# Two transformer blocks on one core: weight items split in halves, the joined product form kept for the FFN ups alone, the recurrence in bursts of four, and two block boundaries with reordered TensorE work

## The chip, the core and the metric

One Trainium2 chip, one core. The metric is device time in microseconds (us) of one execution; the time before is the median of three runs. TensorE runs the matrix products, VectorE (DVE) and ScalarE (ACT) the elementwise work, and the queues of SyncE (SP), ACT and GpSimd (POOL) start DMA transfers.

## The reference, cut to what matters

Two blocks run one behind the other on 256 tokens of width 2048. Block 2 puts 16 meta tokens ahead, so that it has 272 until its attention. Left out here are the normalisations' details, the spatial gating, the pooling and the softmax.

```python
def first_block(x, c, ...):
    mod = silu(c) @ w_ada + b_ada                      # six vectors of 2048
    h = rms_norm(x, g_pre_mix) * (1 + sc1) + sh1
    y = token_mixing(h, w_in, ..., w_out)              # gMLP, attention, pooling
    x = x + gt1 * rms_norm(y, g_post_mix)              # boundary 1
    h = rms_norm(x, g_pre_ffn) * (1 + sc2) + sh2
    y = conv_ffn(h, w_up, w_conv, b_conv, w_down)      # w_up: 2048 x 11264
    return x + gt2 * rms_norm(y, g_post_ffn)           # boundary 2

def second_block(x, meta_tokens, ...):
    h = concatenate([meta, x])
    z = rms_norm_2(h, norm_mix) @ w_in
    q_lat, kv_lat, k_r, u, gates = split(z)
    attn = mla_attention(...)                          # 16 heads, causal
    attn_out = attn @ w_attn_proj                      # w_ap in the kernel
    y = gelu(s5_scan(u, ...))                          # linear recurrence over tokens
    ssm_out = (y @ w_glu_val) * sigmoid(y @ w_glu_gate)
    h = h + (sigmoid(g0) * attn_out + sigmoid(g1) * ssm_out) @ w_out   # boundary 3
    m = rms_norm_2(h, norm_ffn)
    h = h + (silu(m @ w_ffn_gate) * (m @ w_ffn_up)) @ w_ffn_down
    return rms_norm_2(h, norm_final)[:, N_META:]
```

## The kernel before

**Products.** Every fp32 operand is held as a pair, a rounded high part and the rest: a weight is `wh`, `wl`, an activation `act[:, 0]`, `act[:, 1]`. A product is then three: high by high, high by low, low by high. `mm3` (L354) issues three products of 256 columns (L362 to L364; 272 where the meta tokens are in). `mm2` (L366) takes the two with `wh` as one product of 512 columns (L376) and the third as 256 (L378); its two halves of the result have to be added afterwards, by `join` (L380: an ACT copy L382, a DVE add L383). `mmtok` (L386, L394 to L396) has the tokens as rows of the result and 512 columns. `group_unit` and `single_unit` use `mm2`, for the FFN ups of both blocks and for `w_ap`.

**Weights.** A weight item is 1 MB (128 x 2048; some are smaller). SP loads it into one of nine `raw` buffers (L222). `split_piece` (L226) makes the pair: ACT writes `wh` (L249), of which there are four buffers, and DVE `wl` (L250). It does so in two halves of 128 x 1024, or, where the flag `whole` is set, in one piece of 128 x 2048. The flag is set in `block1_in` (L855) and stays set, so nearly all items after the first part of block 1 are split whole.

**Order.** Nothing chooses an order at run time: the program is emitted unit by unit in `run_units` (L322), and every engine does its instructions in that order. A unit (16 values of k by one item, mostly) emits its products, then four stages. Each stage moves the evacuations of the units before by one step (`advance`) and may emit one `split_piece`, in the first two stages only if `whole` is set. Items are split three ahead (`ahead_to`). After the stages two lists of generators are moved on, `side` and `bg`; they carry the attention, the recurrence of s5 and other small work beside the products.

**Boundaries.** At the end of a residual block `tok_block` with `half` (L1080 to L1093) forms the product for the first 128 tokens (a = 0), then for the second (a = 1). Ahead of the evacuation of one of them it splits items of the next stage, `1 + a` of them (L1086). `residual` (L1156) normalises, adds, and for a = 1 returns `dg` (L483), a diagonal of the inverse norms. The next stage's input is made by `lazy_t` (L491), k by k as the first products ask for it: a transpose of the first half (L504), a product of the second with `dg` (L506), at boundary 2 a product of 16 columns for the meta tokens (L508), and then ACT (L512, or L745, L746, L748) and DVE (L513, or L749, L750) write the pair. Boundary 1 is the passage into the first FFN, boundary 2 that into block 2, boundary 3 that into the second FFN.

**The recurrence and its outputs.** 66 steps of eight small DVE operations (L1810 to L1817) run as a `bg` generator that yields after every second step (L1818). Its outputs are PE products of 64 columns (L1846 to L1848), a gelu on ACT (L1852), stores to and loads from DRAM on ACT's queue (L1856, L1863) and a split (L1872, L1873). Attention is emitted by `side` generators in between; its exponentials are L1548, its products L1533, L1534, L1563, L1565 and L1576 to L1578.

```python
                for s in range(stages):
                    self.advance()
                    if self.split < goal and (s < 2 or not self.whole):
                        self.split_piece(self.whole)
```

## Time and profile before

| | |
|---|---|
| median of three runs | 3018.43 us (3017.03 to 3022.11) |
| profiled execution: time, span | 3019.66 us, 3017.9 us |
| PE busy, mean granted clock | 2929.5 us (97% of the span), 0.98 |
| DVE, ACT busy | 2005.8 us (66%), 1391.6 us (46%) |
| matmuls | 17836 |
| HBM read | 632.42 MB, 218 GB/s over the span |
| chain that ended last | PE 92%, DVE 3%, DMA 2%, ACT 2%, issue 1% |

PE is busy nearly throughout and is most of the chain that ended last. The time that could go lies in three places: what the products themselves take, the stretches in which PE stands idle, and those in which the granted clock of TensorE is lower. The granted clock is printed as a share of the full speed: 1.00 is 2.4 GHz, 0.50 is 1.2 GHz.

### The profile page before, as it was taken

How to read it: one execution, taken by the hardware profiler on the slowest of the kernel's cores; microseconds unless marked ns; L12 is line 12 of the kernel's file. 1: busy time of each engine (PE TensorE's matmuls, PEld its weight loads, DVE VectorE, ACT ScalarE, POOL GpSimd, SP SyncE). 2: the span in 40 equal slices, each digit the busy share in tenths (PEclk: the TensorE clock that was granted, in tenths of full speed). 3: DMA queues.
4: the chain of work that ended last, by engine and by line, in shares of the span. 5: the costliest groups of instructions: out<-in, count | busy, mean ns of one | idle time of the engine just before them, and what ended most of it. 6: DMA issues, size and time to landing. Idle time of an engine off the chain costs nothing.

```text
span 3017.9 us, 43503 instructions
## 1 busy us (share of the span) xinstructions
PE 2929.5 (97%) x17836; PEld 2593.5 (86%) x17836; DVE 2005.8 (66%) x2959; ACT 1391.6 (46%) x1878; POOL 56.9 (2%) x109
## 2 busy tenths in 40 slices
PE   6999999989999999999899998999999999999998
PEld 4999989878888888888899996789888888888887
DVE  6889888868779788676436773545645555555454
ACT  4545434456545555455444334434445434444343
POOL 0000000000000100000000000000000000000000
PEclk9999999999999999999899999899999999999999
DMA  9987778775567677556465664246644555555553
GB/s 355 348 302 277 276 269 335 296 257 182 193 241 271 230 268 255 203 180 214 143 220 191 212 209 138 84 162 217 228 179 173 182 198 186 197 183 186 193 190 129
DMA packets 127224, 660.48 MB, mean 219 GB/s; under 512 B 23009, under 2 KB 36065, under 8 KB 57393
## 3 DMA queue, kind: packets, MB, share of 16 engines
q1 hardware_dynamic: 86258, 603.30, 56.0%
q10 hardware_dynamic: 34464, 35.47, 3.7%
q0 software_dynamic: 6304, 18.95, 1.7%
q8 instruction: 140, 2.29, 0.3%
q14 instruction: 58, 0.48, 0.1%
HBM read 632.42 MB, written 25.23 MB: 218 GB/s over the span
## 4 chain that ended last, share of the span: by engine, by line
PE 92%; DVE 3%; DMA 2%; ACT 2%; issue 1%; ACTq 0%; SPq 0%; DVEq 0%
PE pm L376 23%; PE pm L378 12%; PE pm L362 9%; PE pm L363 9%; PE pm L364 9%; PE pm L394 8%; PE pm L396 8%; PE pm L395 8%; DVE wl L250 1%; ACT wh L249 1%; PE pd L506 1%; PE pd L1796 0%; PE pd L1534 0%; PE pd L1732 0%; DMA raw<-w_ada 0%
## 5 line engine op out<-in xcount | busy, mean ns | idle before, releaser
L250 DVE TENSOR_TENSOR wl<-raw,wh 128x2048 fp32r<-128x2048 f32 (+3 forms) x548 | 1092.9, 2006 | 554.1 <-ACT wh L249 553.7
L376 PE MATMUL pm<-act,wh 128*128 128x512 f32 x3072 | 1082.0, 395 | 3.6 <-DVE act L411 2.9
L249 ACT ACTIVATE wh<-raw 128x2048 fp32r<-128x2048 f32 (+3 forms) x548 | 913.2, 1680 | 276.1 <-PE pm L395 148.6
L378 PE MATMUL pm<-act,wl 128*128 128x256 f32 x3072 | 864.4, 281 | 0.0
L362 PE MATMUL pm<-act,wh 128*128 128x256 f32 (+1 forms) x2400 | 690.5, 288 | 8.7 <-DVE hp L842 6.3
L376 PEld LDWEIGHTS pm<-act,wh 128*128 128x128 f32 x3072 | 577.3, 188 | 136.0 <-DVE act L411 3.5
L363 PE MATMUL pm<-act,wh 128*128 128x256 f32 (+1 forms) x2400 | 685.9, 286 | 0.4 <-DVE act L750 0.3
L364 PE MATMUL pm<-act,wl 128*128 128x256 f32 (+1 forms) x2400 | 683.8, 285 | 1.4 <-DVE wl L250 1.4
L378 PEld LDWEIGHTS pm<-act,wl 128*128 128x128 f32 x3072 | 580.2, 189 | 1.2 <-issue 0.7
L362 PEld LDWEIGHTS pm<-act,wh 128*128 128x128 f32 x2400 | 461.0, 192 | 17.8 <-DVE hp L842 6.7
L363 PEld LDWEIGHTS pm<-act,wh 128*128 128x128 f32 x2400 | 460.6, 192 | 1.5 <-DVE act L750 0.7
L364 PEld LDWEIGHTS pm<-act,wl 128*128 128x128 f32 x2400 | 458.8, 191 | 1.8 <-DVE wl L250 1.8
L394 PE MATMUL pm<-wh,act 128*128 128x512 f32 (+1 forms) x1072 | 428.3, 400 | 11.3 <-ACT act L748 5.0
L396 PE MATMUL pm<-wl,act 128*128 128x512 f32 (+1 forms) x1072 | 423.8, 395 | 0.0
L395 PE MATMUL pm<-wh,act 128*128 128x512 f32 (+1 forms) x1072 | 422.8, 394 | 0.8 <-DVE act L750 0.8
L394 PEld LDWEIGHTS pm<-wh,act 128*128 128x128 f32 (+1 forms) x1072 | 201.4, 188 | 62.4 <-ACT act L748 5.6
L395 PEld LDWEIGHTS pm<-wh,act 128*128 128x128 f32 (+1 forms) x1072 | 201.9, 188 | 49.6 <-DVE act L750 1.8
L396 PEld LDWEIGHTS pm<-wl,act 128*128 128x128 f32 (+1 forms) x1072 | 201.3, 188 | 48.6 <-DVE wl L250 0.4
L557 DVE SCALAR_TENSOR_TENSOR raw<-raw,cond 128x2048 f32<-128x2048 f32 x96 | 219.2, 2287 | 5.0 <-DMA raw<-w_ada 4.9
L382 ACT ACTIVATE hp<-pm 128x256 f32<-128x256 f32 x192 | 73.4, 383 | 321.5 <-PE pm L378 320.7
L383 DVE TENSOR_TENSOR hp<-hp,pm 128x256 f32<-128x256 f32 x192 | 80.4, 420 | 115.4 <-ACT hp L382 115.3
L400 ACT ACTIVATE act<-hp 128x256 fp32r<-128x256 f32 x88 | 36.4, 413 | 132.0 <-DVE hp L2025 112.9
(328 smaller groups left out, 1736.9 us busy)
## 6 DMA issues: line engine op xcount, KB each, us to landing
raw<-w_ada SPq DMA_DIRECT2D x96, 1024.0 KB, 5.9
raw<-w_up SPq DMA_DIRECT2D x88, 1024.0 KB, 4.9
raw<-w_ff SPq DMA_DIRECT2D x88, 1024.0 KB, 4.8
raw<-w_in SPq DMA_DIRECT2D x81, 1024.0 KB, 5.2
raw<-w_st SPq DMA_DIRECT2D x37, 1024.0 KB, 6.0
raw<-w_out SPq DMA_DIRECT2D x32, 1024.0 KB, 5.1
raw<-w_down SPq DMA_DIRECT2D x32, 1024.0 KB, 5.0
raw<-w_fd SPq DMA_DIRECT2D x32, 1024.0 KB, 4.9
```

Of the source, the lines that this page charges most:

```text
L249: nc.scalar.activation(vh[:, ks], r[:, ks], AF.Copy)
L250: nc.vector.tensor_tensor(vl[:, ks], r[:, ks], vh[:, ks], op=OP.subtract)
L362: nc.tensor.matmul(o, wh[:, kw, c], x[:, 0, sl], start=start, stop=False, skip_group_check=True)
L363: nc.tensor.matmul(o, wh[:, kw, c], x[:, 1, sl], start=False, stop=False, skip_group_check=True)
L364: nc.tensor.matmul(o, wl[:, kw, c], x[:, 0, sl], start=False, stop=stop, skip_group_check=True)
L376: nc.tensor.matmul(p.rearrange("p (a t) -> p a t", a=2), wh[:, kw, c], x, start=start, stop=False, skip_group_check=True)
L378: nc.tensor.matmul(p[:, T:], wl[:, kw, c], x[:, 0], start=False, stop=stop, skip_group_check=True)
L383: self.nc.vector.tensor_tensor(o, o, p[:, :T], op=OP.add)
L394: nc.tensor.matmul(o, x[:, 0, tok], wh[:, kw], start=start, stop=False, skip_group_check=True)
L395: nc.tensor.matmul(o, x[:, 1, tok], wh[:, kw], start=False, stop=False, skip_group_check=True)
L396: nc.tensor.matmul(o, x[:, 0, tok], wl[:, kw], start=False, stop=stop, skip_group_check=True)
L557: self.nc.vector.scalar_tensor_tensor(o, o, 0.5, self.cond, op0=OP.mult, op1=OP.mult, accum_out=self.m(seg, n))
```

## The change

- `whole` is never set, so every item is split in two halves, and in all four stages of a unit. In the program DVE and ACT have 928 halves of 128 x 1024 each in place of 112, and none of the 392 pieces of 128 x 2048; with the 1536-wide items 408 more instructions on each.
- `mm2` with `join` stays for the FFN ups (`joint=True`). The 16 items of `w_ap` go to `mm3`: 256 pairs of products become 256 triples, 16 joins (ACT and DVE) go, and the gate takes the product from PSUM.
- At the boundaries `tok_block` splits one item ahead of the evacuation, not `1 + a`. Where there are four weight items (boundaries 1 and 3) this is one item in place of two ahead of the second half's evacuation; `group_unit` then splits the next item after its first product.
- `lazy_t` first issues (in `begin`) the transposes of the first half for k = 0 to 2, the sixteen meta products into one tile (with one DVE multiply, and later per k a copy and a subtraction of 16 columns), and `fill` products whose result nothing reads: 20 at boundary 1, none elsewhere. Only then come the products that need `dg`.
- The recurrence yields after every fourth step: 17 bursts of 32 DVE operations in place of 33 of 16. With that its output products are emitted beside units 786 to 799 of the program, which are gate units with 16 values of k, and not beside 803 to 816; attention starts at unit 810 in both.

```diff
--- before.py
+++ after.py
@@ -488,32 +488,61 @@
         q = self.pg(n="jk")[:m, :src.shape[-1]]
         self.nc.scalar.activation(q, src, AF.Square, accum_out=s[:m, col:col + 1])
 
-    def lazy_t(self, src, dg, scale, bias, meta=None):
+    def lazy_t(self, src, dg, scale, bias, meta=None, fill=0):
 
         nc = self.nc
         off = 0 if meta is None else NM
         t = T + off
-        pend, made = {}, {}
+        ps, made, mt = {}, {}, {}
+        def half(k, a):
+            if k not in ps:
+                ps[k] = self.pss()
+            o = ps[k][:, a * 128:a * 128 + 128]
+            i = src[a][k // 4][:, (k % 4) * 128:(k % 4) * 128 + 128]
+            if dg[a] is None:
+                nc.tensor.transpose(o, i, self.ident)
+            else:
+                nc.tensor.matmul(o, i, dg[a], start=True, stop=True, skip_group_check=True)
+        def begin():
+            for k in range(3):
+                half(k, 0)
+            p = self.pss()
+            if meta is not None:
+                for k in range(16):
+                    nc.tensor.matmul(p[:, k * NM:k * NM + NM],
+                                     meta[0][k // 4][:NM, (k % 4) * 128:(k % 4) * 128 + 128], meta[1],
+                                     start=True, stop=True, skip_group_check=True)
+                mt[0] = self.hp(n="mt")[:, :16 * NM].rearrange("p (k t) -> p k t", k=16)
+                nc.vector.tensor_tensor(mt[0], p[:, :16 * NM].rearrange("p (k t) -> p k t", k=16),
+                                        self.vs("norm_mix", 0, 16)[:, :, None].to_broadcast([128, 16, NM]),
+                                        op=OP.mult)
+            w = self.fill_w
+            for _ in range(fill):
+                nc.tensor.matmul(p, w[:, 0, :128], w[:, 0], start=True, stop=True, skip_group_check=True)
 
         def tr(k):
-            p = self.pss()
+            if k == 0:
+                begin()
             for a in range(2):
-                o = p[:, off + a * 128:off + a * 128 + 128]
-                i = src[a][k // 4][:, (k % 4) * 128:(k % 4) * 128 + 128]
-                if dg[a] is None:
-                    nc.tensor.transpose(o, i, self.ident)
-                else:
-                    nc.tensor.matmul(o, i, dg[a], start=True, stop=True, skip_group_check=True)
+                if a or k > 2:
+                    half(k, a)
+            p = ps.pop(k)[:, :T]
+            xt = self.act_tile(t)
             if meta is not None:
-                nc.tensor.matmul(p[:, :NM], meta[0][k // 4][:NM, (k % 4) * 128:(k % 4) * 128 + 128], meta[1],
-                                 start=True, stop=True, skip_group_check=True)
-            xt = self.act_tile(t)
+                nc.vector.tensor_copy(xt[:, 0, :NM], mt[0][:, k])
+                nc.vector.tensor_tensor(xt[:, 1, :NM], mt[0][:, k], xt[:, 0, :NM], op=OP.subtract)
             if bias is None:
-                nc.scalar.activation(xt[:, 0], p[:, :t], AF.Copy, scale=scale(k))
-                nc.vector.scalar_tensor_tensor(xt[:, 1], p[:, :t], scale(k), xt[:, 0].bitcast(FT),
+                nc.scalar.activation(xt[:, 0, off:], p, AF.Copy, scale=scale(k))
+                nc.vector.scalar_tensor_tensor(xt[:, 1, off:], p, scale(k), xt[:, 0, off:].bitcast(FT),
                                                op0=OP.mult, op1=OP.subtract)
             else:
-                self.affine_split(xt, p[:, :t], scale(k), bias(k), k)
+                self.affine_split(xt, p, scale(k), bias(k), k)
+            if k == 15:
+                mt.clear()
             made[k] = xt
 
         def X(k):
@@ -852,7 +881,6 @@
             sprinkle((0.2, 0.6, 0.4)[place])
 
         tm, tp = [None] * 16, [None] * 16
-        self.call(lambda: setattr(self, "whole", True))
 
         def gates(store, base, n4, pump=1):
             for n in range(n4 * 4, n4 * 4 + 4):
@@ -1030,7 +1058,7 @@
                              lambda h: self.q[h // 2] is not None and self.k[h // 2] is not None
                              and None not in self.vatt)
 
-    def group_unit(self, items, X, K, fns, t=T, more=(11, 13)):
+    def group_unit(self, items, X, K, fns, t=T, more=(11, 13), joint=False):
 
 
         lag = 3
@@ -1039,7 +1067,7 @@
             ps = [self.psm() for _ in items]
 
             def mm(i, j):
-                if t == T:
+                if joint:
                     self.mm2(ps[i], self.wt[items[i]], X, j, j == 0, j == K - 1)
                 else:
                     self.mm3(ps[i][:, :t], self.wt[items[i]], X, j, j == 0, j == K - 1)
@@ -1059,11 +1087,14 @@
             return [fn(p) for p, fn in zip(ps, fns)]
         self.unit(items[:1], f, ahead=4)
 
-    def single_unit(self, item, X, K, fn):
+    def single_unit(self, item, X, K, fn, joint=False):
         def f(w):
             p = self.psm()
             for k in range(K):
-                self.mm2(p, w, X, k, k == 0, k == K - 1)
+                if joint:
+                    self.mm2(p, w, X, k, k == 0, k == K - 1)
+                else:
+                    self.mm3(p[:, :T], w, X, k, k == 0, k == K - 1)
             return fn(p)
         self.unit([item], f)
 
@@ -1083,13 +1114,15 @@
                     p = self.psm()
                     tok(ws, ks, a, p)
                     if (a == 1) == (len(ws) == 4):
-                        self.split_to(self.ahead_to(self.split, 1 + a))
+                        self.split_to(self.ahead_to(self.split, 1))
                     self.flush()
                     for _ in fn(a, p):
                         pass
                     half(a)
                 if self.X is not None:
+                    self.fill_w = ws[-1][0]
                     self.X(0)
+                    self.fill_w = None
             self.unit([self.add_item(ap) for ap in items], g, flush=True)
             return
         for i, (ap, kr) in enumerate(zip(items, ks)):
@@ -1184,7 +1217,8 @@
             nc.vector.scalar_tensor_tensor(self.A2, self.mod[:, 64:80], 1.0, self.vs("g_pre_ffn", 0, 16),
                                            op0=OP.add, op1=OP.mult)
         else:
-            self.X, self.made = self.lazy_t(self.x, [None, dg], lambda k: self.A2[:, k:k + 1], lambda k: self.m(3, k))
+            self.X, self.made = self.lazy_t(self.x, [None, dg], lambda k: self.A2[:, k:k + 1], lambda k: self.m(3, k),
+                                            fill=20)
             self.x = self.y = None
 
     def ffn(self, w_up, w_down, upfn, acts, start, evac, tail, late, half):
@@ -1200,9 +1234,9 @@
             if c == 0:
                 n0 = 3
                 self.call(start)
-                self.group_unit(its[:3], X, 16, [upfn(i) for i in range(3)])
+                self.group_unit(its[:3], X, 16, [upfn(i) for i in range(3)], joint=True)
             for i in range(n0, 22):
-                self.single_unit(its[i], X, 16, upfn(c * 22 + i))
+                self.single_unit(its[i], X, 16, upfn(c * 22 + i), joint=True)
                 if c == 3 and i % 5 == 4:
                     self.call(lambda b=i // 5: late(b))
             if c == 3:
@@ -1815,7 +1849,7 @@
             tt(ci, ci, tm[2], op=OP.add)
             tt(cr, cr, tm[1], op=OP.subtract)
             tt(ci, ci, tm[3], op=OP.add)
-            if c % 2:
+            if c % 4 == 3:
                 yield
         self.yS = self.dp.tile([1024, 4, 64], FT, name="yS")
         mts = {}
@@ -1947,11 +1981,8 @@
                         gload(i)
                 if n + 3 < 16:
                     gload(n + 3)
-                v = self.join(p)
-                yield
                 s = gt.pop(n)
-                nc.vector.scalar_tensor_tensor(s, s, 1.0, v, op0=OP.add, op1=OP.mult)
-                v = None
+                nc.vector.scalar_tensor_tensor(s, s, 1.0, p[:, :T], op0=OP.add, op1=OP.mult)
                 yield
                 nc.vector.scalar_tensor_tensor(self.m2[n], self.m2[n], 0.5, s, op0=OP.mult, op1=OP.add)
                 done.add(n)
```

How the instructions stand, at three places. On PE at boundary 1, before (L394 to L396 end block 1; `pd` is the PSUM tile of a transposed k, `x` and `y` the two halves of the tokens; L376 is the FFN's first product):

```order
L395 MATMUL pm_6414<-wh_6312,act_5839 128x512
L396 MATMUL pm_6414<-wl_6313,act_5839 128x512
L504 MATMUL pd_6510<-ident,x_5993 128x128
L506 MATMUL pd_6510<-dg_6508,y_5991 128x128
L504 MATMUL pd_6518<-ident,x_5993 128x128
L506 MATMUL pd_6518<-dg_6508,y_5991 128x128
L504 MATMUL pd_6526<-ident,x_5993 128x128
L506 MATMUL pd_6526<-dg_6508,y_5991 128x128
L376 MATMUL pm_6534<-act_6513,wh_6465 128x512
L378 MATMUL pm_6534<-act_6513,wl_6466 128x256
```

and now (L506 is the transpose, L508 the product with `dg`, L525 the unread product):

```order
L395 MATMUL pm_6526<-wh_6424,act_5927 128x512
L396 MATMUL pm_6526<-wl_6425,act_5927 128x512
L506 MATMUL pd_6614<-ident,x_6089 128x128
L506 MATMUL pd_6616<-ident,x_6089 128x128
L506 MATMUL pd_6618<-ident,x_6089 128x128
L525 MATMUL pd_6620<-wh_6424 128x512 x20
L508 MATMUL pd_6614<-dg_6612,y_6085 128x128
L508 MATMUL pd_6616<-dg_6612,y_6085 128x128
L508 MATMUL pd_6618<-dg_6612,y_6085 128x128
L376 MATMUL pm_6659<-act_6642,wh_6577 128x512
L378 MATMUL pm_6659<-act_6642,wl_6578 128x256
```

The three transposes and 20 products of 512 columns stand ahead of the first instruction that needs `dg`; before, one transpose did.

On PE at boundary 2, before (`me` holds the meta tokens, L362 to L364 are the first item's products):

```order
L504 MATMUL pd_13227<-ident,x_12744 128x128
L506 MATMUL pd_13227<-dg_13225,y_12856 128x128
L508 MATMUL pd_13227<-dg_13128,me_12760 128x16
L504 MATMUL pd_13234<-ident,x_12744 128x128
L506 MATMUL pd_13234<-dg_13225,y_12856 128x128
L508 MATMUL pd_13234<-dg_13128,me_12760 128x16
L504 MATMUL pd_13241<-ident,x_12744 128x128
L506 MATMUL pd_13241<-dg_13225,y_12856 128x128
L508 MATMUL pd_13241<-dg_13128,me_12760 128x16
L362 MATMUL pm_13248<-act_13231,wh_13112 128x272
L363 MATMUL pm_13248<-act_13231,wh_13112 128x272
L364 MATMUL pm_13248<-act_13231,wl_13113 128x272
```

and now (L516 is the meta product):

```order
L506 MATMUL pd_13624<-ident,x_13123 128x128
L506 MATMUL pd_13626<-ident,x_13123 128x128
L506 MATMUL pd_13628<-ident,x_13123 128x128
L516 MATMUL pd_13630<-dg_13525,me_13139 128x16 x4
L516 MATMUL pd_13630<-dg_13525,me_13140 128x16 x4
L516 MATMUL pd_13630<-dg_13525,me_13141 128x16 x4
L516 MATMUL pd_13630<-dg_13525,me_13142 128x16 x4
L508 MATMUL pd_13624<-dg_13622,y_13239 128x128
L508 MATMUL pd_13626<-dg_13622,y_13239 128x128
L508 MATMUL pd_13628<-dg_13622,y_13239 128x128
L362 MATMUL pm_13667<-act_13650,wh_13509 128x272
L363 MATMUL pm_13667<-act_13650,wh_13509 128x272
L364 MATMUL pm_13667<-act_13650,wl_13510 128x272
L506 MATMUL pd_13681<-ident,x_13123 128x128
```

The meta products left the three per-k groups ahead of the first product and, with thirteen more, the groups between the products; all sixteen stand ahead of `dg`.

On ACT beside attention, before (`yt` is an output of the recurrence, `sm` the scores, `qk` an evacuation of queries or keys, `hp` and `pt` other evacuations):

```order
L1852 ACT_TABLE_LOAD
L1852 ACTIVATE yt_17383<-yt_17383 128x512
L1485 ACTIVATE qk_17501<-pm_17488 128x256
L1580 ACTIVATE hp_17507<-pd_17503 128x256
L1567 ACTIVATE pt_17517<-pd_17510 128x384
L1548 ACT_TABLE_LOAD
L1548 ACTIVATE sm_17529,sm_17531<-sm_17529,sm_17531 128x144
L1548 ACTIVATE sm_17529,sm_17531<-sm_17529,sm_17531 128x272
L1856 DMA yS<-yt_17383 32x8x64 x4
```

and now, where attention's exponentials begin (L1906 is the former L1872, L1519 the former L1485, L1582 the former L1548):

```order
L1906 ACTIVATE act_17894<-yD_17862 128x256
L1906 ACTIVATE act_17897<-yD_17864 128x256
L1906 ACTIVATE act_17900<-yD_17866 128x256
L1519 ACTIVATE qk_17916<-pm_17903 128x272
L249 ACTIVATE wh_17920<-raw_17677 128x1024 x2
L1519 ACTIVATE qk_17939<-pm_17926 128x272
L1519 ACTIVATE qk_17954<-pm_17941 128x272
L1519 ACTIVATE qk_17969<-pm_17956 128x272
L1547 ACTIVATE vv_17984<-pm_17971 16x512
L249 ACTIVATE wh_17988<-raw_17778 128x1024 x2
L1582 ACT_TABLE_LOAD
L1582 ACTIVATE sm_17999,sm_18001<-sm_17999,sm_18001 128x144
```

The gelu and its two table loads no longer lie between exponentials; the last s5 work (`act<-yD`) is issued before the first exponential.

## Rows read from the trace of the kernel before

**Rows 1.** The page's first part: busy time, share of the span, instructions per engine.

```profile
PE 2929.5 (97%) x17836; PEld 2593.5 (86%) x17836; DVE 2005.8 (66%) x2959; ACT 1391.6 (46%) x1878; POOL 56.9 (2%) x109
```

**Rows 2.** The waits of PE: who waited for whom, us in total, times, longest.

```profile
PE pd L506 <- DVE dg L483: 18.1, 3, 8.3
PE pm L362 <- DVE hp L842: 6.3, 2, 3.3
PE pm L362 <- DVE pt L842: 1.5, 2, 0.8
```

**Rows 3.** Busy time by stretch: start:end, length, PE, PEld, DVE, ACT, POOL busy, PEclk, DMA share, GB/s.

```profile
668.50:673.10 4.60, 4.05 (x15) 3.60 (x16) 2.37 (x5) 2.32 (x5) 1.74 (x4) 0.50 0.44 131
1448.70:1471.90 23.20, 23.19 (x88) 20.57 (x89) 8.51 (x13) 7.60 (x13) 0.00 (x0) 0.50 0.16 57
1782.50:1792.70 10.20, 7.59 (x36) 7.59 (x36) 9.93 (x37) 0.00 (x0) 0.00 (x0) 0.50 0.78 284
1837.10:1850.70 13.60, 12.11 (x39) 8.46 (x39) 5.18 (x18) 7.41 (x17) 1.08 (x2) 0.50 0.34 110
1884.90:1891.60 6.70, 6.67 (x22) 4.42 (x20) 3.48 (x8) 4.70 (x10) 0.00 (x0) 0.50 0.00 0
1895.10:1908.70 13.60, 13.60 (x48) 10.16 (x46) 4.01 (x14) 4.20 (x14) 1.08 (x2) 0.50 0.22 87
2178.90:2181.80 2.90, 2.90 (x7) 2.25 (x8) 1.58 (x4) 2.90 (x6) 0.00 (x0) 0.50 1.04 396
```

**Rows 4.** The same view, the attention's stretch and the first FFN.

```profile
690.00:1230.00 540.00, 540.00 (x2929) 465.70 (x2928) 440.44 (x630) 297.61 (x426) 33.89 (x63) 1.00 0.66 235
1780.00:1910.00 130.00, 114.84 (x621) 92.01 (x621) 59.28 (x151) 49.06 (x95) 3.24 (x6) 0.83 0.41 137
```

**Rows 5.** The same view, 60 us with `mm3` alone and with `mm2` alone.

```profile
2016.00:2076.00 60.00, 60.00 (x507) 60.00 (x506) 31.81 (x31) 24.07 (x22) 0.00 (x0) 1.00 0.60 206
2100.00:2160.00 60.00, 60.00 (x346) 52.58 (x345) 40.42 (x50) 24.95 (x23) 0.00 (x0) 1.00 0.66 237
```

**Rows 6.** Timeline of boundary 1: start, us, engine line op, out<-in, count.

```profile
658.09 4.63 DVE L250 TENSOR_TENSOR wl<-raw,wh 128x1024 fp32r<-128x1024 f32 x4 [1.13 <-ACT wh L249]
660.80 0.57 ACT L489 ACTIVATE jk<-pm 128x512 f32<-128x512 f32 x1
662.64 0.69 DVE L1130 TENSOR_TENSOR y<-pm,gp 128x512 f32<-128x512 f32 x1
```

**Rows 7.** Timeline of boundary 2: a weight load for meta tokens and the next one.

```profile
1454.32 0.50 PEld L508 LDWEIGHTS pd<-dg,me 16*128 16x128 f32 x2 [0.22 <-issue]
1454.86 0.29 PEld L362 LDWEIGHTS pm<-act,wh 128*128 128x128 f32 x1
```

**Rows 8.** Timeline: the recurrence on DVE beside gate units.

```profile
1639.89 0.20 DVE L1810 TENSOR_TENSOR tm<-X,a 128x32 f32<-128x32 f32 x1
1640.88 0.22 DVE L1810 TENSOR_TENSOR tm<-X,a 128x32 f32<-128x32 f32 x1
1643.35 2.29 DVE L250 TENSOR_TENSOR wl<-raw,wh 128x2048 fp32r<-128x2048 f32 x1 [1.39 <-ACT wh L249]
```

**Rows 9.** Groups of ACT by line in 1780:1910: count, busy us, mean ns, idle before.

```profile
L1852 ACT ACT_TABLE_LOAD x3 | 3.8, 1283 | 0.1
```

**Rows 10.** One piece of the chain in 1860:1900: start, us, what.

```profile
1868.90 5.84 DMA yD<-yS
```

**Rows 11.** Timeline ahead of boundary 3, where the `x2d` loads are issued.

```profile
2172.18 6.20 ACTq L1153 DMA_DIRECT2D x<-x2d  x7
...
2178.89 0.80 PE L394 MATMUL pm<-wh,act 128*128 128x512 f32 x1 [2.86 <-ACT act L413]
```

**Rows 12.** Groups by form: the splits, count, busy us, mean ns, idle before.

```profile
L249 ACT ACTIVATE wh<-raw 128x2048 fp32r<-128x2048 f32 x392 | 746.7, 1908 | 158.3 <-PE pm L395 108.1 <-issue 19.0 <-DMA raw<-w_out 12.1
L249 ACT ACTIVATE wh<-raw 128x1024 fp32r<-128x1024 f32 x112 | 112.4, 1049 | 53.3 <-DMA raw<-w_st 25.5 <-PE pm L363 14.1 <-DVE raw L557 7.6
...
L250 DVE TENSOR_TENSOR wl<-raw,wh 128x2048 fp32r<-128x2048 f32 x392 | 897.3, 2291 | 501.4 <-ACT wh L249 501.2
```

## The prediction

> **What bounds the kernel now.** I read the page first: PE is busy for 97% of the span [rows 1], so only three things can pay: fewer or shorter products, less idle time of PE, or a higher granted clock. Then the waits of PE, to see where it idles [rows 2]; the largest is `dg`, 18.1 us in three waits, one per boundary, the longest 8.3 at boundary 1. Then busy time by stretch at the places where PE had just been idle: in each of them the granted clock is 0.50, the lower level (1.2 GHz), while elsewhere it is 1.00 [rows 3, 5]. So a gap is paid twice, as idle time and as the slow products behind it. Attention has most of both: from 1780 to 1910 PE is busy 114.84 of 130 us, at a mean clock of 0.83 [rows 4]. The sum is made against the profiled execution, 3019.66 us; the median of three is 1.23 lower. A measurement of this kernel can tell about 0.2% (6 us) from no change.
>
> **The change part by part.**
>
> *Half splits in block 1.* DVE evacuations there stand behind whole 2.29 us subtractions [rows 8, 12]; PE waits 6.3 us on `hp` and 1.5 on `pt` of L842 [rows 2]. Behind a half the wait is at most 1.16 us long (4.63 for four [rows 6]), so the `pt` waits of up to 0.8 go, -1.5, and of the `hp` waits I take a quarter, -1.5. Together **-3.0**; bounds 0 (the waits are for something behind the splits) and -6 (half of `hp` too).
>
> *Half splits elsewhere.* A half costs 1049 ns on ACT where a whole item costs 1908 [rows 12]: 190 more per item. In the first FFN, where DVE is fullest, it is busy 440 of 540 us and ACT 298 [rows 4], and PE never waits. Before the whole subtractions DVE sits 501 us waiting for ACT's `wh` [rows 12]; with halves it starts after half of that. The cover is the lead of three items; I take **0**.
>
> *Boundary 1.* Four halves in a row keep DVE until 662.72 (658.09 + 4.63), and ACT's sum of squares starts at 660.80; the chain to `dg` goes on at 662.64 [rows 6]. With two halves in place of four it can go on about 1.75 earlier (the two that go take 2.3 us on DVE; ACT and the last product then set the start): -1.75. Three transposes no longer stand in the path behind `dg`: -0.4. The 20 unread products take 20 x 0.23 = 4.6 us (two thirds of a `mm2` pair of 0.347, [rows 5]) in a gap that is still 6.6 us: nothing on the path. If they keep the clock, the 4.05 us of work at 0.50 behind the gap [rows 3] halve, -2.0 at most; if the clock falls among them, they take 9.2 us and PE is 3 us late. I take -1.0. Next is late: the second item is now split behind k = 0, and its two halves, 2.3 us on DVE, stand before the input of k = 3, with three pairs of products (1.04 us) for cover: +1.3. Sum **-1.9**, bounds +3 and -4.
>
> *Boundary 2.* A meta product of one k costs PE 0.22 us before and 0.54 until the next weight load [rows 7], 0.76 at half clock. Thirteen of the sixteen lie in the half-clock stretch that ends at 1471.9 [rows 3], three behind it at, by estimate, half the price: -9.9 and -1.2. All sixteen move into the idle 7.4 us (18.1 less 8.3 and the 2.4 of boundary 3), where they need 4.3 us at full and 8.6 at half clock, by the 0.54: between 0 and +1.6, I take 0. Without them 13.3 of the 23.2 us at half clock are left. At boundary 1, where the groups per k are the same but for the meta products, the clock was back after 4.6 us [rows 3]. I take 6 us here, near that row: -(13.3 - 6)/2 = -3.7, bounds 0 and -4.4. The six small DVE operations that the first three k gain cost +0.7 (eight take 0.99, [rows 8]). Sum **-14.1**, bounds -8 and -17.
>
> *S5 and attention.* The output products, the gelu, the stores and loads of s5 move from attention's units (4 values of k each, little time to hide anything) to gate units of 16. That takes the 5.84 us yD transfer [rows 10] out of ACT's queue in attention, where the splits, and so the scores, stood behind it, and the table loads between gelu and exponential (three of 1.28 us each way, the gelu's in [rows 9]). PE's 15.2 idle us in that stretch [rows 4] shrink, I take to 3, left for scores that wait behind a split: -12.2. The four half-clock stretches are 44.1 us long with 40.0 of work [rows 3]; at full clock that is 20.0 less. Sum **-32.2**, bounds -18 (half the gaps stay, and each takes the clock down) and -36.
>
> *Bursts of four.* One step takes 0.99 us on DVE [rows 8], so four with a split 3.96 + 2.32 = 6.28, where a gate unit on PE takes 48 products of 118 ns, 5.67 (60 us for 507, [rows 5]). If nothing covers this, 17 bursts cost 17 x 0.61 = +10.4. The lead of three items (some 17 us) covers it: with two steps DVE still waits 1.39 us per unit [rows 8]. I take **0**, bounds 0 and +10.4.
>
> *`w_ap` with three products.* 60 us hold 507 products of `mm3` or 346 of `mm2` [rows 5], 355 ns for a triple and 347 for a pair: 256 x 8 ns = +2.0. The joins go, and with them the order in which ACT did a join and a whole `wh` ahead of the last x2d loads, 6.20 us in its queue, behind which the next input was late by 2.86 us [rows 11]: -2.9, and 2.9 us of work at half clock [rows 3]: -1.4. Sum **-2.3**, bounds +2 and -4.
>
> *Boundary 3.* Transposes -0.4, the later split +1.3 as at boundary 1, no unread products: **+0.9**, bounds 0 and +2.
>
> Sum: -3.0 + 0 - 1.9 - 14.1 - 32.2 + 0 - 2.3 + 0.9 = -52.6. 3019.66 - 52.6 = 2967.1, and I forecast **2967** (the 1.23 to the median is within the choices above).
>
> **A rule against the filling.** From 1448.7 to 1471.9 PE is busy 23.19 of 23.20 us, and the granted clock stays at 0.50 all the while [rows 3]; at boundary 1 it is back after 4.6. So a busy PE did not bring the clock back there. The Trainium skill ("TensorE: Matmul & The Clock Gate", Part 4: PE-mode transpose) says that transposes do not count as busy for the clock gate in the way that products do. By it the transposes pulled into the gaps would hold no clock.
>
> **The rivals.**
> 1. *The transposes, not the meta products, hold the clock down.* Then both boundaries keep their slow stretch: +3.7 at boundary 2 and +1.0 at boundary 1, 2972. For it: 1448.7 to 1471.9 has a transpose in every group. Against it: so has boundary 1, which came back after 4.6 us. Chance 0.15. By the page's rule this is what would happen; the trace so far speaks for it at one place and against it at the other.
> 2. *Bursts make DVE the bound beside the gates*, 2967 + 10 = 2977. For it 6.28 against 5.67; against it the lead of three items. 0.12.
> 3. *Attention keeps half of its gaps.* Its scores still wait behind splits, and a remaining gap takes the clock down: 2967 + 14 = 2981; with rival 2 as well, 2991. For it: units of 4 values of k give splits little cover with or without s5. 0.17.
> 4. *The change doesn't do what it says*: the s5 work does not get out of attention, because the recurrence still ends late. Then only boundaries and `w_ap` pay, 2967 + 32 = 2999. The order of the program speaks against it. 0.04.
> 5. *Halves lose the lead of the splits.* Place: ACT in the units with 16 values of k; price 392 items x 190 ns = +74 on the path, 3019.66 - 52.6 + 74 = 3041, slower than before. It decides once splits take longer than the unit they lead, 2.1 + 2.4 us against 5.55; the 501 us for which DVE waits and the full PE from 690 to 1230 [rows 4, 12] speak against it. 0.03.
>
> **How the numbers follow.** The forecast has 0.49, its own range 2955 to 2978. The range of 8 in 10 takes in rivals 1 to 3, whose latest is 2991, and at the low end the far bounds of block 1, the boundaries and attention together (-3, -2, -3 and -4, with 2 of `w_ap`), about 2953: 2950 to 2992. Faster by over 0.2% is everything but rival 5 and half of what lies between, 0.95; within 0.2% 0.02; slower 0.03.
>
> **What would show it.** Right: the waits of PE in attention's stretch down to a few us and a clock near 1.00 there; no meta products between the products behind boundary 2 and its half-clock stretch under 8 us; a `dg` wait at boundary 1 under 3 us with unread products in front; no gap of PE at the last x2d loads; DVE's waits for `wh` far below 501 us. Wrong: PE waiting for L250 in FFN units (rival 5), for L250 or `X` beside the gates (rival 2), for `sm` in attention (rival 3), or 0.50 over 13 us behind boundary 2 (rival 1).

## The result, and the profile after

The changed kernel takes 2969.8 us (median of four, 2969.13 to 2974.38) against 3017.73 (four runs, 3013.36 to 3022.11): ratio 0.9844, 95% interval 0.9827 to 0.9862, 48 us less. The forecast was 2967, range 2950 to 2992. The profiled execution took 2974.38 us (span 2972.3, clock 0.992), the longest of the four; against its counterpart of before, 3019.66, it is 45.3 us shorter, where the sum, made against that execution, had 52.6.

The same instructions of PE can be found in both traces, so the span divides into stages without any model. A stage is that of the one profiled execution of its kernel. The times, in us, that begin the stages are: the start of the first of 480 triples in block 1; the end of the last L396 ahead of boundary 1; the first `mm2` pair behind the last transpose there; the same two at boundary 2 (with L362); the run of 576 triples that leads into `w_ap`; the first L394 of the last output product of block 2; its last L396's end; the first `mm2` pair behind boundary 3's transposes; the end of the last product.

| stage | before | after | length, before to after | forecast |
|---|---|---|---|---|
| block 1 | 74.53 | 75.52 | 585.56 to 582.20: -3.4 | -3.0 |
| boundary 1 | 660.09 | 657.72 | 28.26 to 26.98: -1.3 | -1.9 |
| first FFN | 688.36 | 684.71 | 751.65 to 751.65: 0 | 0 |
| boundary 2 | 1440.01 | 1436.36 | 44.47 to 29.45: -15.0 | -14.1 |
| block 2 to `w_ap` | 1484.48 | 1465.81 | 525.64 to 498.36: -27.3 | -32.2 |
| `w_ap` | 2010.12 | 1964.17 | 161.41 to 163.85: +2.4 | -2.3 with the next |
| output product | 2171.53 | 2128.01 | 93.56 to 88.55: -5.0 | |
| boundary 3 | 2265.09 | 2216.56 | 21.50 to 24.32: +2.8 | +0.9 |
| second FFN | 2286.58 | 2240.89 | 723.10 to 723.28: +0.2 | 0 |

Four rows of the waits of PE, after (columns as in [rows 2]):

```profile
PE pd L508 <- DVE dg L483: 7.4, 3, 3.5
...
PE pm L362 <- DVE hp L871: 4.8, 2, 2.6
...
PE pm L394 <- ACT qk L1519: 2.1, 1, 2.1
...
PE pd L1567 <- DVE sm L1575: 0.9, 1, 0.9
```

The wait for `dg` is 7.4 us in place of 18.1 [rows 2]; most of that is not time won, since 4.8 us of unread products and 3.7 of meta products now fill it. The waits for `hp` are down by a quarter, and no wait for X or for `pmt` is among them any more; the longest of attention is 2.1 us. Before, the longest two there were:

```profile
PE pd L1847 <- DVE X L1816: 4.8, 1, 4.8
PE pd L1565 <- DVE sm L1541: 4.1, 1, 4.1
```

Busy time by stretch, after (columns as in [rows 3]), the half-clock stretches and, last, attention:

```profile
667.00:670.40 3.40, 3.40 (x14) 3.12 (x15) 3.34 (x6) 3.25 (x6) 0.00 (x0) 0.50 0.11 37
1441.80:1448.60 6.80, 3.54 (x14) 3.30 (x15) 4.77 (x17) 5.17 (x14) 1.83 (x4) 0.50 0.46 169
1796.80:1800.20 3.40, 3.40 (x10) 1.54 (x8) 3.28 (x9) 1.87 (x6) 0.00 (x0) 0.50 0.19 77
1820.70:1824.10 3.40, 3.40 (x14) 2.96 (x14) 1.69 (x6) 1.88 (x7) 0.54 (x1) 0.50 0.50 200
2220.00:2226.90 6.90, 6.26 (x25) 5.71 (x25) 4.99 (x8) 4.08 (x8) 0.00 (x0) 0.51 0.24 72
1780.00:1910.00 130.00, 126.20 (x731) 98.12 (x730) 78.72 (x174) 63.84 (x145) 5.94 (x11) 0.97 0.36 123
```

In attention PE is busy 126.20 of 130 us at a clock of 0.97, where it was 114.84 at 0.83 [rows 4]. But the clock still fell there twice, for 3.4 us each. Boundary 2 has 6.8 us at half clock, 3.5 of them busy, where 23.2 busy ones were [rows 3]; boundary 3 has 6.9.

Boundary 1 in the timeline, after:

```profile
655.72 2.36 DVE L250 TENSOR_TENSOR wl<-raw,wh 128x1024 fp32r<-128x1024 f32 x2 [1.12 <-ACT wh L249]
...
657.81 4.83 PE L525 MATMUL pd<-wh 128*128 128x512 f32 x20
...
658.48 0.69 DVE L1163 TENSOR_TENSOR y<-pm,gp 128x512 f32<-128x512 f32 x1 [0.40 <-ACT jk L489]
...
664.58 0.94 PE L508 MATMUL pd<-dg,y 128*128 128x128 f32 x6 [1.94 <-DVE dg L483]
...
666.85 0.65 PE L376 MATMUL pm<-act,wh 128*128 128x512 f32 x1 [1.34 <-DVE act L779]
```

Two halves end on DVE at 658.08, and the chain goes on at 658.48, 0.9 us behind the start of PE's transposes at 657.56. Before, it went on at 662.64 [rows 6], 2.7 us behind the first transpose:

```profile
659.93 0.27 PE L504 MATMUL pd<-ident,x 128*128 128x128 f32 x1
```

The 20 unread products fill 4.8 us. The first pair starts 9.1 us behind the last product of block 1 (657.72 to 666.85); before it was 11.0.

Boundary 2, PE alone, after:

```profile
1437.31 0.55 PE L506 MATMUL pd<-ident,x 128*128 128x128 f32 x3 [0.94 <-DVE x L1207]
1437.78 3.74 PE L516 MATMUL pd<-dg,me 16*128 16x16 f32 x32
1445.06 1.65 PE L508 MATMUL pd<-dg,y 128*128 128x128 f32 x6 [3.54 <-DVE dg L483]
```

All sixteen meta products (two records each) take 3.74 us in a row, 0.23 each, at full clock, in a gap that has 3.54 us to spare behind them.

What the chain of waits names at the first gap left in attention, after:

```profile
1788.58 4.18 DMA yD<-yS
...
1794.46 0.64 ACT act L1906
1795.10 0.29 ACT qk L1519
1795.43 0.41 PE pm L394
```

The s5 outputs are no longer between the scores, but the last of their loads still lands just ahead of attention's first product units: behind the 4.18 us transfer come the last `act` pieces and one `qk` on ACT, and PE waits 2.1 us for that. ACT's table loads from 1500 to 1945 us, six before (three of them in [rows 9]), are now two:

```profile
L1886 ACT ACT_TABLE_LOAD x1 | 1.3, 1283 | 0.0
L1582 ACT ACT_TABLE_LOAD x1 | 1.3, 1283 | 0.0
```

### The profile page after: what moved, and what is told of

It reads as the page before. It is cut to its first block, busy times and chain, and to the rows that moved or that the text cites. A ratio compares the mean times of both kernels' runs of the same rounds, so it can differ in the third digit from the quotient of the medians.

```text
span 2972.3 us, 44890 instructions
## 1 busy us (share of the span) xinstructions
PE 2911.2 (98%) x18112; PEld 2591.0 (87%) x18112; DVE 2029.2 (68%) x3400; ACT 1420.2 (48%) x2282; POOL 56.9 (2%) x109
## 4 chain that ended last, share of the span: by engine, by line
PE 91%; DVE 6%; ACT 1%; DMA 1%; issue 1%; ACTq 0%; SPq 0%; DVEq 0%
PE pm L376 22%; PE pm L378 11%; PE pm L362 9%; PE pm L363 9%; PE pm L364 9%; PE pm L394 8%; PE pm L396 8%; PE pm L395 8%; DVE wl L250 2%; PE pd L1568 1%; PE pd L1567 1%; PE pd L508 0%; PE pd L1830 0%; PE pd L1766 0%; DMA raw<-w_ada 0%
## 5 line engine op out<-in xcount | busy, mean ns | idle before, releaser
L250 DVE TENSOR_TENSOR wl<-raw,wh 128x1024 fp32r<-128x1024 f32 (+1 forms) x972 | 1132.9, 1196 | 396.7 <-ACT wh L249 394.5
L249 ACT ACTIVATE wh<-raw 128x1024 fp32r<-128x1024 f32 (+1 forms) x972 | 962.4, 1031 | 322.3 <-PE pm L395 119.7
L376 PE MATMUL pm<-act,wh 128*128 128x512 f32 x2816 | 993.4, 396 | 2.0 <-DVE act L779 1.3
L378 PE MATMUL pm<-act,wl 128*128 128x256 f32 x2816 | 792.7, 282 | 0.0
L362 PE MATMUL pm<-act,wh 128*128 128x256 f32 (+1 forms) x2656 | 757.6, 285 | 9.2 <-DVE hp L871 4.8
L363 PE MATMUL pm<-act,wh 128*128 128x256 f32 (+1 forms) x2656 | 754.1, 284 | 1.6 <-DVE act L411 1.0
L364 PE MATMUL pm<-act,wl 128*128 128x256 f32 (+1 forms) x2656 | 751.8, 283 | 1.1 <-DVE wl L250 1.1
L376 PEld LDWEIGHTS pm<-act,wh 128*128 128x128 f32 x2816 | 529.8, 188 | 123.1 <-ACT act L775 1.5
L362 PEld LDWEIGHTS pm<-act,wh 128*128 128x128 f32 x2656 | 505.6, 190 | 18.4 <-DVE hp L871 5.6
L363 PEld LDWEIGHTS pm<-act,wh 128*128 128x128 f32 x2656 | 504.6, 190 | 3.5 <-DVE act L411 1.9
L364 PEld LDWEIGHTS pm<-act,wl 128*128 128x128 f32 x2656 | 502.5, 189 | 1.7 <-DVE wl L250 1.7
L394 PE MATMUL pm<-wh,act 128*128 128x512 f32 (+1 forms) x1072 | 428.8, 400 | 11.7 <-ACT act L777 5.8
L396 PE MATMUL pm<-wl,act 128*128 128x512 f32 (+1 forms) x1072 | 424.6, 396 | 0.0
L394 PEld LDWEIGHTS pm<-wh,act 128*128 128x128 f32 (+1 forms) x1072 | 201.5, 188 | 63.6 <-ACT act L777 6.4
L396 PEld LDWEIGHTS pm<-wl,act 128*128 128x128 f32 (+1 forms) x1072 | 201.7, 188 | 49.1 <-issue 0.6
L382 ACT ACTIVATE hp<-pm 128x256 f32<-128x256 f32 x176 | 67.2, 383 | 351.5 <-PE pm L378 351.1
L383 DVE TENSOR_TENSOR hp<-hp,pm 128x256 f32<-128x256 f32 x176 | 73.6, 419 | 208.3 <-ACT hp L382 208.3
L2067 DVE TENSOR_TENSOR x<-pm,x 128x512 f32<-128x512 f32 x32 | 22.1, 692 | 91.3 <-PE pm L396 91.3
```

Of the source, the lines that this page charges most:

```text
L249: nc.scalar.activation(vh[:, ks], r[:, ks], AF.Copy)
L250: nc.vector.tensor_tensor(vl[:, ks], r[:, ks], vh[:, ks], op=OP.subtract)
L362: nc.tensor.matmul(o, wh[:, kw, c], x[:, 0, sl], start=start, stop=False, skip_group_check=True)
L363: nc.tensor.matmul(o, wh[:, kw, c], x[:, 1, sl], start=False, stop=False, skip_group_check=True)
L364: nc.tensor.matmul(o, wl[:, kw, c], x[:, 0, sl], start=False, stop=stop, skip_group_check=True)
L376: nc.tensor.matmul(p.rearrange("p (a t) -> p a t", a=2), wh[:, kw, c], x, start=start, stop=False, skip_group_check=True)
```

## The experiments

Twelve kernels, each timed in at least four executions. "Stage" is one of the table above, taken at the same instructions. The changed kernel's 2969.8 was not timed beside the experiments; the kernel before was, and had medians of 3016.8, 3015.3, 3016.0 and 3019.5, so differences under some 4 us are left to the stages.

**Bursts and halves, each undone and each alone.** Four kernels: the changed one with bursts of two, or with whole splits; the one before with bursts of four alone, or with halves alone.

```diff
-            if c % 4 == 3:
+            if c % 2:
                 yield
```

> The changed kernel (2969.8 us) with the recurrence yielding after every second step again; halves and everything else stay. My theory (the bursts take s5's outputs out of attention's units): the recurrence ends 16 units later, its output products lie beside attention again, PE waits some 4 us for X and a few us for scores, and half-clock stretches come back there: 2985 to 2997. Rival (longer bursts only load DVE, and it is the half splits that freed attention): 2960 to 2971, no wait for X.

```diff
         tm, tp = [None] * 16, [None] * 16
+        self.call(lambda: setattr(self, "whole", True))
```

> The changed kernel with the flag for whole splits set again. My theory: about 3 us in block 1 come back and the two waits behind whole pieces in attention grow a little: 2973 to 2985. Rival (halves cost 190 ns more per item on ACT and that is paid on the path): 2969.8 - 60 to -10, faster than the changed kernel. Second rival (halves are what cleared attention): 2990 or more.

The other two are the same lines the other way, in the kernel before.

> The kernel before (3017.7 us) with nothing changed but the yield after every fourth step. My theory: most of the gain in attention comes from this one line: 2988 to 2999, no wait for X, table loads of ACT beside attention two in place of six. Rival (DVE becomes the bound beside the gates, 0.61 us in each of 17 units): 3028.

> The kernel before with nothing changed but that the flag for whole splits is never set. My theory: block 1 gives 3 us and attention something, since splits there stand behind shorter pieces; the s5 outputs stay beside attention: 2998 to 3015. Rival (halves on the path, slower side): 3020 to 3040.

| kernel | us | ratio to before | block 1 | block 2 to `w_ap` |
|---|---|---|---|---|
| before | 3017.7 | 1 | 585.6 | 525.6 |
| halves alone | 3005.4 | 0.9958 (0.9945 to 0.9971) | 581.9 | 524.9 |
| bursts of four alone | 3003.1 | 0.9957 (0.9943 to 0.9971) | 587.1 | 504.5 |
| changed, bursts of two | 2994.6 | 0.9927 (0.9901 to 0.9953) | 582.1 | 519.7 |
| changed, whole splits | 2982.4 | 0.9889 (0.9868 to 0.9911) | 588.1 | 504.8 |
| changed | 2969.8 | 0.9844 (0.9827 to 0.9862) | 582.2 | 498.4 |

In the stage up to `w_ap` bursts alone give -21.2, halves alone -0.7, both -27.3. The stages of halves alone are those of the slowest of its ten executions (3010.25 us; the median is 3005.4), those of bursts alone of the fastest of its eight, so the two totals lie closer than their stages. The waits of PE between 1500 and 1945 us show what the bursts do. Halves alone:

```profile
PE pd L1575 <- DVE pmt L1567: 4.1, 1, 4.1
PE pd L1846 <- DVE X L1815: 4.1, 1, 4.1
```

Bursts of four alone:

```profile
PE pm L394 <- ACT qk L1485: 1.9, 1, 1.9
PE pd L1533 <- DVE sm L1541: 1.7, 1, 1.7
...
PE pm L364 <- DVE wl L250: 0.7, 3, 0.3
```

The changed kernel with bursts of two:

```profile
PE pd L1610 <- DVE pmt L1602: 4.2, 1, 4.2
PE pd L1881 <- DVE X L1850: 4.1, 1, 4.1
PE pd L1599 <- DVE sm L1575: 2.5, 1, 2.5
```

With bursts of two PE waits for X (L1846, L1847 and L1881 are the product with X), for `pmt` and for `sm`, whatever the splits are like; ACT has its six table loads there. With bursts of four no wait there is longer than 2.4 us in these kernels, none is for X, and ACT has two. The halves add another 6 us in that stage with bursts of four (504.8 to 498.4), and 3 to 6 us in block 1. Beside bursts of two they give 0.7 or 6: the stage takes 524.9 us in the one kernel with both and 519.7 in the other, with the same code there and 44.4 and 34.1 us at half clock. So it is not shown that the halves need the bursts. The rival that halves would lose on the path is out: the first FFN takes 751.65 us with halves and with whole splits. The bursts alone miss the expected range by 4 us with their median of eight; the profiled execution among them, 2996.8 us, lies in it, and what the others lost is not known.

**Bursts of eight**, to see what covers longer bursts.

```diff
-            if c % 4 == 3:
+            if c % 8 == 7:
                 yield
```

> The changed kernel (2969.8 us) with the recurrence yielding after every eighth step: 9 bursts in 9 gate units. My theory is a balance over the whole recurrence: 66 steps take 65 us on DVE and each gate unit's splits 2.4 more; over 9 units that is 87 us of DVE work in 51 us of PE work, 36 short, of which the lead of three items covers some 17, so PE waits about 19 us for wl (L364 on L250), and its clock falls in some of these waits: 2987 to 2997. (Bursts of four: 106 in 96, 10 short, within the lead; bursts of two: 143 in 187.) Rival (the lead does not matter, since waits of DVE for wh are what gives way): PE waits under 5 us, 2965 to 2975.

2989.7 us, 0.9912 (0.9881 to 0.9942). The waits of PE from 1590 to 1700 us, then busy time of 1600 to 1670:

```profile
PE pm L364 <- DVE wl L250: 17.9, 7, 4.2
```

```profile
1600.00:1670.00 70.00, 52.11 (x351) 50.65 (x349) 70.00 (x427) 16.37 (x23) 0.00 (x0) 0.85 0.42 142
```

The balance gave 19 us of waits and they are 17.9; DVE is busy for all of the 70 us, and the clock falls six times among them (0.85 on the mean). That agrees with the reading that bursts of four are free because their shortage of 10 us fits into the lead of the splits, and not because DVE has time beside each unit. The lead itself was not varied.

**The meta products back in the loop.**

```diff
-            if meta is not None:
-                for k in range(16):
-                    nc.tensor.matmul(p[:, k * NM:k * NM + NM],
...
+            if meta is not None:
+                nc.tensor.matmul(ps[k][:, :NM], meta[0][k // 4][:NM, (k % 4) * 128:(k % 4) * 128 + 128], meta[1],
+                                 start=True, stop=True, skip_group_check=True)
```

> The changed kernel (2969.8 us) with the sixteen meta products of boundary 2 back in the loop over k; the early transposes stay. My theory: they cost 0.76 us each at half clock and 0.4 at full, so 16 of them 6 to 12 us, plus a half-clock stretch that ends later: 2978 to 2984; stretch from the boundary's first transpose to the gate units' stage 8 to 14 us longer. Rival (the long half-clock stretch of the profiled run before was that run's chance, and the products cost their full-clock price): 2973 to 2977.

2983.4 us, 0.989 (0.9872 to 0.9908), as expected; the small DVE operations of the meta tokens go with the edit. The stage of boundary 2 is 40.64 us against 29.45, +11.2. Its half-clock stretch, and then that of the kernel with bursts of four alone, in which the loop is the old one:

```profile
1437.30:1457.80 20.50, 14.56 (x53) 12.72 (x54) 10.02 (x19) 8.50 (x19) 2.17 (x4) 0.50 0.43 157
```

```profile
1445.10:1458.80 13.70, 9.86 (x36) 8.38 (x36) 7.31 (x13) 7.22 (x16) 2.17 (x4) 0.50 0.33 108
```

Four kernels have the meta products in the loop: half clock for 13.7, 17.1 (halves alone), 20.5 and, before, 27.3 us (23.2 of it with PE busy, [rows 3]), stage 38.75, 39.94, 40.64 and 44.47. The ten that have them early: stretches of 6.8 or 10.2 us or two of 3.4, and a stage of 29.45 to 29.49 in nine of them (30.72 in the one with more unread products). So the part is worth 9 to 11 us against the other three profiles, and the 15 of the profiled pair hold a stretch of 27 us that is longer than in any of them. The early transposes do not show: this kernel has them and takes no less than the two that do not (38.75 and 39.94).

**Two-product form for `w_ap` again.**

```diff
+                v = self.join(p)
+                yield
...
-            self.single_unit(its[n], X, 16, fn(n))
+            self.single_unit(its[n], X, 16, fn(n), joint=True)
```

> The changed kernel with the two-product form and join for the 16 items of w_ap again. My theory: products 2.0 us shorter, the wait at the x2d loads comes back at most in half (half splits ahead of the loads in ACT's queue): 2968 to 2972, no difference that can be told. Rival (the joins caused the wait of 2.86 us and the clock's fall behind it): 2973 to 2976.

2968.8 us, 0.9847 (0.9827 to 0.9867): not to be told from the changed kernel. `w_ap` is 1.8 us shorter, the output product 2.1 longer (162.10 and 90.66). The input behind the x2d loads, ACT in the timeline:

```profile
2127.20 1.03 ACT L413 ACTIVATE act<-m 128x256 fp32r<-128x256 f32 x3 [2.84 <-issue]
```

It starts at 2127.20 and PE waits 1.51 us for it, with its clock at 1.00; before it was 2.86 us and the clock fell [rows 11]. Of ACT, before, the last join ahead of those loads, and then the changed kernel with whole splits, which has no joins:

```profile
2171.73 0.39 ACT L382 ACTIVATE hp<-pm 128x256 f32<-128x256 f32 x1 [2.48 <-PE pm L378]
```

```profile
2134.76 6.12 ACTq L1187 DMA_DIRECT2D x<-x2d  x8
2140.92 1.04 ACT L413 ACTIVATE act<-m 128x256 fp32r<-128x256 f32 x3 [4.25 <-DMA x<-x2d]
```

The join waits for the last product of `w_ap`, and the loads stand behind it in ACT's order (2171.8 on, where the output product starts at 2171.53). Without joins they are issued 5.6 us ahead of that product (it starts at 2140.36), and PE has no wait there, whole splits or halves (the output product takes 88.65 and 88.55 us). With joins the wait is 2.9 us with whole splits and 0.5 (halves alone) or 1.5 with halves. So the joins are what makes the wait, and the halves alone would have taken half of it or more.

**That form, with the x2d loads on GpSimd's queue**, an attempt at a better kernel.

```diff
-            self.x = self.load_tok(self.x2d)
+            self.x = self.load_tok(self.x2d, self.nc.gpsimd)
```

> The changed kernel with the two-product form for w_ap again and the eight x2d loads ahead of boundary 3 issued on GpSimd's queue, not ACT's. My theory: the wait at those loads (1.5 us in the kernel with the two-product form) goes, and the products' 1.8 us are won: 2966 to 2968. Rival (the joins themselves are late, or GpSimd's issue brings the data too late for the residual): 2970 or more, with a new wait in the block output.

2973.5 us, 0.9864 (0.9847 to 0.9881): the rival. GpSimd's queue, then the waits of PE from 2025 to 2050 us:

```profile
2027.44 2.16 POOL L1186 DMA_DIRECT2D x<-x2d  x4 [63.35 <-PE pm L364]
```

```profile
PE pm L376 <- DVE act L411: 6.0, 3, 2.7
```

The same waits with the loads on ACT's queue:

```profile
PE pm L376 <- DVE act L411: 3.0, 3, 1.4
```

GpSimd's queue, which has nothing else in this stretch, issues the last five loads at 2027 to 2030.5, each time when PE (L364) releases what they waited for. That is some 95 us sooner than on ACT's queue, and just where `w_ap` asks for its first inputs; these come 3.0 us later in all, the clock falls (2037.8 to 2044.6), and `w_ap` takes 167.6 us, not 162.1. Whether the transfers or GpSimd's issuing delayed the inputs was not separated.

**No unread products at boundary 1, and transposes in their place.**

```diff
-                                            fill=20)
+                                            fill=0)
```

> The changed kernel without the 20 unread products at boundary 1. My theory: PE idles 6.6 us there, its clock falls in the gap, and the work behind it runs at half clock for some 4 us: +1 to +2, 2970 to 2972. Rival (they hold no clock, since it falls behind the gap either way): within 0.5 us in the stretch of boundary 1.

```diff
-                nc.tensor.matmul(p, w[:, 0, :128], w[:, 0], start=True, stop=True, skip_group_check=True)
+                nc.tensor.transpose(p[:, :128], src[0][0][:, :128], self.ident)
```

(with 54 of them)

> The changed kernel with 54 transposes of 128 columns in place of the 20 unread products, about as long. If transposes keep the clock as products do, the stretch behind boundary 1 looks like the changed kernel's (half clock for 3.4 us). If they do not, it looks like the kernel's without any filling: half clock from the middle of the filling on, 7 us or more, and the transposes themselves take longer once it falls: 2970 to 2974.

2971.8 us, 0.9854 (0.9838 to 0.987), and 2968.9, 0.9845 (0.9827 to 0.9862); the stage of boundary 1 is 27.31 and 26.99, against 26.98. Without filling, busy time by stretch:

```profile
660.60:665.00 4.40, 0.00 (x0) 0.00 (x0) 3.00 (x7) 2.85 (x9) 3.31 (x7) 0.50 0.96 375
665.00:670.80 5.80, 4.83 (x18) 4.28 (x19) 4.25 (x7) 4.87 (x9) 1.55 (x3) 0.50 0.42 145
```

With transposes:

```profile
657.50:663.90 6.40, 6.37 (x58) 6.13 (x56) 4.31 (x9) 3.82 (x12) 2.75 (x6) 1.00 0.95 370
663.90:667.10 3.20, 1.27 (x8) 1.06 (x9) 1.88 (x6) 2.07 (x6) 2.11 (x4) 1.00 0.83 284
667.10:670.50 3.40, 3.40 (x15) 3.03 (x13) 3.37 (x5) 3.06 (x5) 0.00 (x0) 0.51 0.01 5
```

The idle PE is at half clock from 660.6. With 54 transposes, 6.37 of 6.40 us busy, it is granted 1.00 throughout, and through the 3.2 us of waits and a few products behind them, until 667.1; then come 3.4 us at half clock, as in the changed kernel from 667.0. So here transposes held a full clock as products did; whether they would bring it back from half was not tried. The filling is worth 0.3 us in the stage, as the rival had it; the total of 2971.8 cannot be told from 2969.8.

Nor do the 3.4 us at half clock behind the filling cost anything. The kernel with the two-product form, with the same 20 unread products, kept 1.00 through this boundary:

```profile
654.87:666.00 11.13, 7.86 (x43) 6.40 (x42) 7.69 (x17) 7.56 (x19) 4.87 (x9) 1.00 0.80 295
667.90 0.51 PE L376 MATMUL pm<-act,wh 128*128 128x512 f32 x1 [1.62 <-DVE act L779]
```

Its stage is 26.99 us all the same: PE then waits 1.62 us for the input of k = 3. So does the kernel with the meta products in the loop (26.98).

**More unread products.**

```diff
-                                            fill=20)
+                                            fill=26, more=5)
...
+            if k == 2:
+                idle(more)
```

> The changed kernel with more unread products: 26 ahead of dg at boundary 1, 6 at boundary 2, 7 at boundary 3, and 5, 4, 4 more behind the products with dg of k = 2, where PE waits for the first input. My theory: no gap is long enough for the clock to fall, so the half-clock stretches of 3.4, 6.8 and 3.4 to 6.9 us behind the three boundaries go, 1.7 to 3.4 us each: 2962 to 2967. Rival (the filling reaches past the moment at which dg or the input is ready, or the clock falls among it): PE is late by what it wins, 2969 to 2974.

2970.4 us, 0.9852 (0.9837 to 0.9867): the rival. Boundary 1 and the stretch among boundary 2's filling, busy time:

```profile
655.70:667.00 11.30, 9.56 (x49) 7.47 (x47) 8.26 (x17) 8.11 (x19) 4.88 (x9) 1.00 0.69 258
1438.40:1441.80 3.40, 2.90 (x7) 1.79 (x6) 2.16 (x6) 2.78 (x9) 2.15 (x4) 0.50 0.72 259
```

Boundary 1 in the timeline:

```profile
663.74 0.47 PE L376 MATMUL pm<-act,wh 128*128 128x512 f32 x1 [0.18 <-DVE act L786]
...
667.64 0.51 PE L376 MATMUL pm<-act,wh 128*128 128x512 f32 x1 [1.62 <-DVE act L786]
```

The clock stays at 1.00 through boundary 1, and the stage is 27.01 us against 26.98. What the faster products win is lost at 667.64, where PE waits 1.62 us for the input of k = 3, which stands on DVE behind the split of the second item. In the changed kernel the products ahead of it run at half clock, without that wait, and PE is at k = 3 just as late: 13.0 us behind the last product of block 1 in both. At boundary 2 the filling ran partly at half clock, and the stage is 1.3 us longer; that the one is the cause of the other was not separated.

**Two items ahead at the boundaries again.**

```diff
-                        self.split_to(self.ahead_to(self.split, 1))
+                        self.split_to(self.ahead_to(self.split, 1 + a))
```

> The changed kernel (2969.8 us) with two items split ahead of the second half's evacuation at boundaries 1 and 3 again, not one. My theory: the wait for dg at boundary 1 grows from 1.9 to about 3.7 us, and the wait of 1.6 us for the fourth input behind it goes, so the two cancel: stretch of boundary 1 within 0.7 us of the changed kernel's 27.15, total 2968 to 2973. Rival (the order of the splits was what the boundary gained by): stretch 1.5 to 2 us longer.

2972.2 us, 0.9856 (0.9842 to 0.9871); boundary 1 is 29.02 us, 2.0 longer, boundary 3 22.55, 0.5 to 0.7 shorter than the 23.03 to 23.27 of seven experiments with the changed kernel's code there. The rival is right at boundary 1:

```profile
662.42 1.25 PE L508 MATMUL pd<-dg,y 128*128 128x128 f32 x6 [3.53 <-DVE dg L483]
```

The wait for `dg` is 3.53 us, about as expected, and the first pair starts 10.7 us behind the last product of block 1, not 9.1. The wait ahead of k = 3 is gone, but that pair does not come sooner in return, 14.55 us behind that product for 13.03: PE was at half clock until 669.7, and that work now lay on the path.

## Why the prediction was right

The forecast is 2.8 us from the measured median, and part of that is luck: on the pair of executions that the sum was made for it is 7.3 us too much, 52.6 for 45.3, and the terms below miss in both directions.

*Half splits in block 1*: -3.4 for -3.0; the `pt` waits are gone and the `hp` waits a quarter shorter, as reckoned.

*Half splits elsewhere* was put at 0, and that is too little: in attention they give 6 us beside bursts of four (504.8 with whole splits, 498.4 with halves). One of the signs named for it came only in part: DVE's waits for `wh` went from 553.7 us over all splits (501.2 of it for the whole pieces, [rows 12]) to 394.5, which is not far below.

*Boundary 1*: the first product comes 1.9 us sooner; the estimate for `dg` and the transposes was 2.15. The clock term was 0.3 for 1.0, because the input of k = 3 is late at either clock: the wait put at +1.3 is 1.62 us at full clock. The stage gives -1.3 for -1.9.

*Boundary 2*: -15.0 for -14.1 is luck in part. The sum priced thirteen products at half clock because this one profile had them there for 27 us; in three other kernels with the same loop the stretch was 14 to 21 us. The measured worth is 9 to 11 us.

*S5 and attention* is the term that was mis-sized most: -27.3 for -32.2. The mechanism held: no wait for X, no yD in attention's queue but at its beginning, six table loads down to two. The idle part came out: over the stage 16.3 us went to 4.1, and between 1780 and 1910, where the sum left 3, 3.8 are there. The miss of 4.9 is in the clock. That part was put at -20.0, with no half clock left; but PE's busy time in the stage went from 509.4 to 494.2 us, -15.1. Two stretches of 3.4 us at half clock make 2.8 of the difference, and such stretches come and go: five experiments with the same code in this stage (the two on the two-product form, transposes as filling, more unread products, two items ahead) have none, with no less idle time (4.6 to 5.4 us), and PE is busy for 491.3 to 491.5. The other 2 are a price: even there the 40 us at half clock were worth 18, not 20. *Bursts* at 0 was right, and the run with eight agrees with the lead as the cover.

*`w_ap`*: -2.6 over both stages for -2.3. The 2.0 us of longer products are there (+1.8). The 4.3 us for the joins are there as well (-5.0 in the output product), and the kernel with whole splits shows the order that was named for them. But the halves overlap with it: with them in place the joins are worth 2.1 us, not 4.3.

*Boundary 3*: +2.8 for +0.9. Seven experiments with the same code there take 23.03 to 23.27 us, with 3.4 us at half clock or none, against 24.32 with 6.9: some 1.1 to 1.3 are that longer stretch. The rest is +1.5 to +1.8 against this profile of before; two other kernels with the old code there took 22.60 and 23.10, so how much the edit costs is open.

Of the rivals, the one on the transposes has fallen: the stretch behind boundary 2 is 6.8 us long with a transpose in each group, and 54 transposes kept the clock at 1.00. The Trainium skill ("TensorE: Matmul & The Clock Gate", Part 4: PE-mode transpose) has it the other way, that transposes do not count as busy in the same way; for holding a full clock the measurement here decides, from one trace. That DVE would become the bound beside the gates is true of bursts of eight, not of four. Attention kept 3.8 of its 15.2 idle us, not half. No run beat the changed kernel: the two below it (2968.8 and 2968.9) cannot be told from it.

## What to carry to other kernels

Where small serial work shares an in-order engine with large pieces, sum both over the whole stretch against the work they feed and compare the shortage with the lead: that told bursts of four and eight apart. Before filling a gap to keep the clock, look at what the next products wait for; where their inputs are late anyway, the lower clock is free. And price a stretch at half clock from more than one trace.

## What was not expected

Stages that no edit touched differ between kernels: the time to the start of the first stage is 70.4 to 76.5 us and the second FFN 722.2 to 726.2, while the first FFN is 751.65 or 751.66 in all but one of them (751.64). The runs do not say why; a difference of a few us in a total proves nothing without its stage, and a stage of one profile little without a second.
